# 32 steps of the second half's input projection ahead of the first half's mixers

## The chip, the cores and the metric

The kernel runs on one core of one Trainium2 chip. The metric is the device time of one execution in microseconds, median over several. A core has TensorE (PE, matrix multiply), VectorE (DVE), ScalarE (ACT), GpSimd (POOL) and SyncE (SP), which here issues the DMA transfers. Each engine takes its instructions strictly in the order in which they were put on it; an instruction that waits holds everything behind it on its engine.

## The reference

One step of a decoder layer over 2048 prompt tokens and 64 sample tokens (8 sequences of 8), model width 1024. Cut to what matters:

```python
h = rmsnorm(x) * (1 + sc1) + sh1
proj = h @ w_in                               # 1024 -> 2816 columns
qkv, z, b, a, sq, sk, sv = split(proj)
qkv = silu(causal_conv4(qkv))
o_dn = gated_delta_rule(qkv, b, a)            # 4 heads of 128, chunk by chunk
o_dn = rmsnorm(o_dn) * silu(z)
o_swa = window_attention(sq, sk, sv)          # 8 heads, window 128, sinks, bias
x = x + g1 * (concat(o_dn, o_swa) @ w_out)
h = rmsnorm(x) * (1 + sc2) + sh2
u = causal_conv3(h @ w_up)                    # 2 x 2816
x = x + g2 * ((silu(gate) * up) @ w_down)
y = rmsnorm(x)
```

## The kernel before, in words

Activations lie transposed, columns are tokens. All large products are split in three: an operand is a high part `hi` and a remainder `lo`, and one k of 8 takes three matmuls on PE, hi by hi, lo by hi, hi by lo. That is one *step* of a projection (`gemm_steps`). The tokens come in two halves: the first has two blocks of 512 columns, the second three of 384, 384 and 320 (`HALVES`), the last 64 of which are the sample tokens.

The input projection (`inproj`) has 22 weight tiles of 128 output columns. `project` takes pairs of weight tile m and block in the order that `pairs` gives: for the second half the first two weight tiles go together over the blocks, so that the order is (m0, b0), (m1, b0), (m0, b1), (m1, b1), (m0, b2) and so on. Each pair fills one PSUM tile `in_ps` in eight steps, 24 matmuls, from a pool of two banks, and `in_evac` then takes it away: for m below 12 a convolution of four taps (`conv_block`: ACT L538 and L541, three DVE L548), SiLU (L565, L566) and a store to `proj`.

The activations of the second half come from `affine_h`, called by `second` when the first half's projection has let a block's place go. For each block and k a tile `ht` is loaded (SP L264), scaled (DVE L265), and split into `hi` (ACT) and `lo` (DVE L272 or POOL L269 by turns). The 64 sample columns are loaded together as `hst` (SP L249) and worked on in four DVE steps (L252 to L256). `ht`, `hst` and the evacuations' `ev` share one tag, "cv", of five buffers.

The mixers of the first half (`mixers(0, mp)`) run chunks 0 to 7. For each chunk four generators go in lockstep: the state recurrence `scan` (s_ps, o_ps, p_ps), attention `attend` (as_ps, pt_ps, pv_ps; it loads kw, qs and sv), the triangular inverse of the next chunk `levels` (z_ps, u_ps, small tiles), and `front` two chunks ahead (kq_ps, d_ps, v_ps, am_ps; vb at L699 scales the values). `beside(steps, filler, share)` issues `share` filler steps behind each mixers step; `SHARE[1]` is 2.0, and the filler is the second half's input projection. When the mixers have been issued, `between(0, ...)` loads their result (`mix_load`: mt from `mixd`, split at L1171 and L1172) beside the rest of the in-projection (`in_end`), and then the out-projection (op_ps) begins.

The order in the program is a priority and not the order on the engines. The framework schedules ahead of time: by its own estimate of what is ready it picks, on each engine, the earliest instruction in the program that can go, and that fixes each engine's order. So what stands earlier in the program tends to go first where both are ready.

Of the kernel before, what the change touches and what calls it, by code (L numbers as in the profile page):

```python
# [96 lines left out]
def kernel(  # L97
# [7 lines left out]
    def new_pool(es, name, bufs=1, side="left", space=None):  # L105
        kw = {} if space is None else dict(space=space)
        return es.enter_context(tc.tile_pool(name=name, bufs=bufs, side=side, reuse_waits="tile", **kw))
# [218 lines left out]
    def load_split(src, eng=None, out=None):  # L326
        return split(load_raw(src), eng, out)
# [22 lines left out]
    def beside(steps, filler, share):  # L350

        due = 0.0
        for _ in steps:
            due += share
            while due >= 1:
                next(filler, None)
                due -= 1

    def lockstep(*gens):
        gens = list(gens)  # L360
        while gens:
            gens = [g for g in gens if next(g, None)]
            yield True
# [5 lines left out]
    def rest(steps):  # L369
        for _ in steps:  # L370
            pass

    def project(ms, src, load, hb, hf, evac, after=None, freed=None, tags=("acc",), turn=(2, 2), third=None, w0=None):


        order = list(pairs(ms, turn, len(HALVES[hf])))
        new = [m for i, (m, _) in enumerate(order) if m not in [x for x, _ in order[:i]]]
        first = max(2, turn[0])
        w = {m: w0 if w0 and not i else (load, third)[i == 2](m) for i, m in enumerate(new[:first])}
        new = new[first:]  # L380
        last = {bi: i for i, (_, bi) in enumerate(order)}
        for i, (m, bi) in enumerate(order):
            ps = bank(src, tags[i % len(tags)])
            yield from gemm_steps(ps, w[m], hb[bi], HALVES[hf][bi][1])
            end = bi == len(HALVES[hf]) - 1
            if end and new:
                w[new[0]] = load(new[0])
                new.pop(0)
            evac(m, bi, ps)
            if end and after:  # L390
                after(m)
            if freed and last[bi] == i:
                freed(bi)
# [197 lines left out]
    def in_evac(hf, bi, m, ps, ic):  # L591
        c0, n = HALVES[hf][bi]
        np_ = n - LS if c0 + n == LT else n
        ev = evp[0].tile([P, 512], F32, tag="cv", name="ev", bufs=evp[2])[:, :n]
        if m < 12:
            o = ic["out"]
            rb = conv_block(ps, n, np_, o[:, m, 0:3], b8(o[:, m, 3:27]), ic["cw"][:, m], None, ev)
            if TWICE[hf] == 2:
                silu2(ev, rb)
            else:  # L600
                nc.scalar.activation(ev, ev, AF.Silu)
        elif m < 16:
            nc.scalar.activation(ev, ps[:, :n], AF.Tanh, scale=0.5)
            nc.vector.scalar_tensor_tensor(ev, ev, 1.0, ps[:, :n], ALU.add, ALU.mult)  # L604
            nc.gpsimd.tensor_scalar(ev, ev, ic["dnw"], 1.0, ALU.mult, ALU.mult)
        elif m < 20:
            nc.scalar.mul(ev, ps[:, :n], -0.125)
        else:
            nc.scalar.copy(ev, ps[:, :n])
        nc.sync.dma_start(proj[m, :, c0:c0 + n], ev)  # L610
        if m == 20 and c0 + n == LT:
            nc.sync.dma_start(O["p_swa_k"], ev[:, np_ - P:np_])
            nc.sync.dma_start(O["s_swa_k_new"], ev[:, np_:])

    def inproj(hf, h, ic, ms, **kw):
        return project(ms, "in_ps", lambda m: load_split(I["w_inT"][m], nc.gpsimd if hf and m % 2 else nc.vector), h, hf,
                       lambda m, bi, ps: in_evac(hf, bi, m, ps, ic), **kw)
# [9 lines left out]
    def attn_consts(pool):  # L627
        NB = pool.tile([P, 8, P], F32, tag="NB", name="NB", bufs=1)
        t0 = toep[0]
        for v in range(2):  # L630
            t = pool.tile([P, 4, 256], F32, tag="kq", name="nbt", bufs=3)
            nc.sync.dma_start(t, bass.AP(t0.tensor, t0.offset + 4 * v * P * TOEP + 127, [[TOEP - 1, P], [P * TOEP, 4], [1, 256]]))
            nc.vector.tensor_tensor(NB[:, 4 * v:4 * v + 4], t[:, :, :P], t[:, :, P:], ALU.min)
        own = pool.tile([P, P], F32, tag="own_", name="own_", bufs=1)
        nc.vector.tensor_tensor(own, cst[:, C_TGT:C_TGT + P], ident, ALU.add)
        sink = pool.tile([P, 8], F32, tag="sink", name="sink", bufs=1)
        nsink = pool.tile([P, 8], F32, tag="nsink", name="nsink", bufs=1)
        nc.sync.dma_start(sink, I["sinks"].partition_broadcast(P))
        nc.vector.tensor_scalar_mul(nsink, sink, -1.0)
        return NB, own, sink, nsink  # L640
# [125 lines left out]
    def inverse_tiles(pool):  # L766

        inv[:] = [pool.tile([P, H, P], F32, tag=f"inv{i}", name=f"inv{i}", bufs=1) for i in range(2)]
        inv.append(pool.tile([P, H, 64], F32, tag="T64", name="T64", bufs=1))
        for t in inv:  # L770
            nc.gpsimd.memset(t, 0.0)
# [147 lines left out]
    def attend_load(c, pool):  # L919
        c0, k0 = P * c, P * (c == 0)  # L920

        qs = pool.tile([P, 4, P], F32R, tag="qs", name="qs", bufs=1)
        nc.sync.dma_start(qs.bitcast(F32), proj[16:20, :, c0:c0 + P].rearrange("m p t -> p m t"))
        kw = pool.tile([P, 256], F32R, tag="kw", name="kw", bufs=1)
        nc.sync.dma_start(kw[:, k0:].bitcast(F32), proj[20, :, c0 - P + k0:c0 + P])
        sv = pool.tile([P, P], F32, tag="sv", name="sv", bufs=1)
        nc.sync.dma_start(sv, proj[21, :, c0:c0 + P])
        return qs, kw, sv
# [456 lines left out]
    class Quarters:  # L1385
# [14 lines left out]
        def ahead(self, p, j):  # L1400

            J, end = len(self.order), MI - 1 - PLAIN
            i = J * (p - PLAIN) + j + RING
            if i < J * end:
                self.split(PLAIN + i // J, i % J)
            else:
                self.split(MI - 1, i - RING_T - J * end)
# [468 lines left out]
    with ExitStack() as main:  # L1876
# [95 lines left out]
        filler = inproj(0, h, ic, range(2, 12), tags=("acc", "acc", "fr", "fr", "at"), turn=(0, 0), w0=w2)  # L1972
# [16 lines left out]
        def mixers(hf, pool):  # L1989
            c0 = NCH // 2 * hf  # L1990
            c1 = c0 + NCH // 2
            ds = chunks
            at = attn_consts(pool)
            loaded = [attend_load(c0, pool)]
            for c in range(c0, c1):
                g = [scan(c, ds[c], pool), attend(c, c1, at, loaded, pool)]
                if c + 1 < c1:
                    g.append(levels(ds[c + 1], pool))
                if c + 2 < c1:
                    g.append(front(c + 2, ds[c + 2], pool))  # L2000
                yield from lockstep(*g)
# [10 lines left out]
        with ExitStack() as es:  # L2012
            mp = new_pool(es, "mp", bufs=2, side="right")
            filler = inproj(0, h, ic, range(12, 22), freed=second, turn=(0, 2))
            inverse_tiles(mp)
            beside(ahead(0, mp), filler, SHARE[0])
            rest(filler)
            g1 = gates(1, h1, ic["wb"], ip)
            filler = inproj(1, h1, ic, range(22), after=lambda m: m in range(2, 20) and next(g1, None))
            beside(mixers(0, mp), filler, SHARE[1])  # L2020
        uc = []

        def in_end():
            yield from filler
            nc.sync.dma_start(O["dn_conv"], ic["out"])
            states.close()
            uc.append(up_consts(new_pool(states, "up")))

        with ExitStack() as es:
            up_tags[:] = FREE_TAGS  # L2030
            filler, _ = between(0, in_end(), es, range(MU))
# [10 lines left out]
        with ExitStack() as es:  # L2042
            up_tags[:] = FREE_TAGS
            filler, h = between(1, filler, es, range(2 * PLAIN))
# [119 lines left out]
```

## Time and profile before

| | |
|---|---|
| median of 3 runs | 2659.92 us (2656.89 to 8718.18) |
| profiled execution | 2661.34 us |
| its span | 2659.2 us |
| mean granted TensorE clock | 0.99 |
| PE busy | 2583.2 us (97%), 16552 instructions |
| DVE busy | 1828.3 us (69%) |
| ACT busy | 1262.5 us (47%) |
| POOL busy | 752.7 us (28%) |

The span runs from the first to the last instruction of the profiled execution. Within it the mixers of the first half begin at about 355 us, their last matmul (ot_ps) is at 739.2 us, and the last in_ps of the second half ends at about 810 us, where the out-projection begins. Rows of the timeline give the start, the duration, the engine, the line, the operation, out<-in, and in square brackets the idle time before with what ended it.

### The profile page before, as it was taken

To read this page: it belongs to the slowest core of one execution; us is meant where nothing else is said; L and a number is where in the kernel's file an instruction comes from. 1 tells how busy PE (TensorE), PEld (TensorE's weight loads), DVE (VectorE), ACT (ScalarE), POOL (GpSimd) and SP (SyncE) were. 2 spreads that over 40 slices of the span, in tenths; PEclk is the share of its full clock that TensorE was granted. 3 is DMA by queue.
4 is the path that set the end of the run, shared out by engine and by line. 5 is a ranking of instruction groups with operands and counts; after the bars stand their busy time and mean duration, and the time that the engine had idled before them with its cause. 6 is when DMAs were issued, how large, how long until landed. Compare 5 with 4: busy or idle time off the path is not lost. (4 is left out here: it accounts for less than half of the span.)

```text
span 2659.2 us, 45647 instructions
## 1 busy us (share of the span) xinstructions
PE 2583.2 (97%) x16552; PEld 2231.5 (84%) x16552; DVE 1828.3 (69%) x3681; ACT 1262.5 (47%) x3081; POOL 752.7 (28%) x643
## 2 busy tenths in 40 slices
PE   6999989999999899999999999999999999999998
PEld 5677877887898787777777779999999997889988
DVE  6475469988422678878857665786777666677676
ACT  5453255555232445545444454555555553554343
POOL 2032134332331422323111113345555520021022
PEclk9999989999999999999999999999999999999999
DMA  7787343332255343333226447424555458678673
GB/s 278 247 302 233 114 128 114 86 101 85 87 167 182 116 136 87 84 102 95 77 86 202 148 156 245 135 74 154 172 175 183 167 183 293 211 237 283 218 247 133
DMA packets 305791, 433.58 MB, mean 163 GB/s; under 512 B 81779, under 2 KB 189012, under 8 KB 305300
## 3 DMA queue, kind: packets, MB, share of 16 engines
q1 hardware_dynamic: 305564, 430.66, 49.7%
q8 instruction: 130, 2.13, 0.3%
q14 instruction: 97, 0.79, 0.1%
HBM read 316.25 MB, written 115.33 MB: 162 GB/s over the span
## 5 line engine op out<-in xcount | busy, mean ns | idle before, releaser
L340 PE MATMUL in_ps<-hi,w_hi 128*128 128x512 f32 (+2 forms) x880 | 317.6, 364 | 9.5 <-DVE ev L604 4.7
L340 PE MATMUL up_ps<-hi,w_hi 128*128 128x512 f32 (+2 forms) x808 | 316.4, 392 | 7.3 <-ACT cv L543 7.3
L340 PE MATMUL in_ps<-lo,w_hi 128*128 128x512 f32 (+2 forms) x880 | 318.4, 362 | 2.7 <-DVE lo L272 1.7
L340 PE MATMUL in_ps<-hi,w_lo 128*128 128x512 f32 (+2 forms) x880 | 315.9, 359 | 0.0
L340 PE MATMUL up_ps<-lo,w_hi 128*128 128x512 f32 (+2 forms) x808 | 312.9, 387 | 0.0
L340 PE MATMUL up_ps<-hi,w_lo 128*128 128x512 f32 (+2 forms) x808 | 311.7, 387 | 0.0
L1784 PE MATMUL dn_ps<-th,wh 128*128 128x512 f32 (+2 forms) x796 | 272.3, 343 | 5.4 <-DVE x L1252 3.5
L1784 PE MATMUL dn_ps<-tl,wh 128*128 128x512 f32 (+2 forms) x796 | 272.6, 343 | 3.5 <-DVE tl L1676 3.5
L1784 PE MATMUL dn_ps<-th,wl 128*128 128x512 f32 (+2 forms) x796 | 271.2, 342 | 0.0
L332 DVE TENSOR_TENSOR w_lo<-w_raw,w_hi 128x1024 fp32r<-128x1024 f32 x115 | 143.4, 1247 | 110.8 <-ACT w_hi L331 109.0
L331 ACT CAST w_hi<-w_raw 128x1024 fp32r<-128x1024 f32 x126 | 132.1, 1048 | 161.6 <-PE op_ps L340 58.7
L340 PEld LDWEIGHTS in_ps<-hi,w_hi 128*128 128x128 f32 x880 | 166.7, 190 | 31.9 <-issue 5.1
L340 PEld LDWEIGHTS up_ps<-hi,w_hi 128*128 128x128 f32 x808 | 152.3, 188 | 46.3 <-issue 11.4
L340 PEld LDWEIGHTS in_ps<-lo,w_hi 128*128 128x128 f32 x880 | 167.1, 190 | 26.6 <-issue 7.6
L340 PEld LDWEIGHTS in_ps<-hi,w_lo 128*128 128x128 f32 x880 | 167.1, 190 | 16.1 <-issue 1.6
L340 PEld LDWEIGHTS up_ps<-lo,w_hi 128*128 128x128 f32 x808 | 152.4, 189 | 33.2 <-issue 8.5
L340 PEld LDWEIGHTS up_ps<-hi,w_lo 128*128 128x128 f32 x808 | 152.3, 189 | 30.6 <-issue 4.0
L1784 PEld LDWEIGHTS dn_ps<-th,wh 128*128 128x128 f32 x796 | 150.9, 190 | 22.6 <-DVE x L1252 4.8
L1784 PEld LDWEIGHTS dn_ps<-tl,wh 128*128 128x128 f32 x796 | 151.1, 190 | 19.4 <-DVE tl L1676 3.8
L1784 PEld LDWEIGHTS dn_ps<-th,wl 128*128 128x128 f32 x796 | 151.0, 190 | 15.5
L1675 ACT CAST wh<-wr 128x512 fp32r<-128x512 f32 x149 | 92.1, 618 | 144.8 <-PE dn_ps L1784 113.9
L548 DVE SCALAR_TENSOR_TENSOR ev<-rb,cw,ev 128x512 f32<-128x512 f32 (+2 forms) x180 | 131.4, 734 | 26.9 <-ACT ev L541 25.1
(546 smaller groups left out, 6488.5 us busy)
## 6 DMA issues: line engine op xcount, KB each, us to landing
w_raw<-in_w_upT_dram SPq DMA_DIRECT2D x50, 512.0 KB
wada<-in_w_ada_dram SPq DMA_DIRECT2D x48, 512.0 KB
w_raw<-in_w_inT_dram SPq DMA_DIRECT2D x44, 512.0 KB
wr<-ws_d SPq DMA_DIRECT2D x88, 256.0 KB
w_raw<-in_w_outT_dram SPq DMA_DIRECT2D x34, 512.0 KB
d<-act_d SPq DMA_DIRECT2D x33, 512.0 KB
wr<-in_w_downT_dram SPq DMA_DIRECT2D x66, 256.0 KB
tr<-T_d SPq DMA_DIRECT2D x66, 256.0 KB
```

Of the source, the lines that this page charges most:

```text
L331: nc.scalar.copy(hi, raw)
L332: (eng or nc.vector).tensor_tensor(lo, raw, hi.bitcast(F32), ALU.subtract)
L340: nc.tensor.matmul(ps[:, :n], a[:, k, :], b[:, k, :n], start=first is not False and k == ks[0] and i == 0, stop=last is not False and k == ...
L548: nc.vector.scalar_tensor_tensor(out, src(j), w[:, j:j + 1], out, ALU.mult, ALU.add)
L1675: nc.scalar.copy(h, raw)
L1784: nc.tensor.matmul(acc[m, s][:, :n], w[q, i][a][:, c], th[b][:, v], start=new and i == 0 and y == 0, stop=i == KH - 1 and y == 2, skip_gro ...
```

## The change

Between the making of the filler and `beside`, 32 filler steps are issued at once, then the mixers begin as before.

```diff
             g1 = gates(1, h1, ic["wb"], ip)
             filler = inproj(1, h1, ic, range(22), after=lambda m: m in range(2, 20) and next(g1, None))
+            for _ in range(32):
+                next(filler)
             beside(mixers(0, mp), filler, SHARE[1])
```

A PSUM tile takes eight steps, so these are four tiles: weight tiles 0 and 1 on the first block and on the second. No instruction is added or taken away on any engine; only the order differs. The orders agree up to the start of the mixers, differ from there to the end of the in-projection, and agree again from the out-projection's first matmul on.

On PE, at the start of the first half's mixers, before: two in_ps steps stand between the inverse (z_ps), and the attention scores (as_ps) and the recurrence (s_ps) follow.

```order
L780 MATMUL z_ps<-T_2270,AM 32x16 x5
L340 MATMUL in_ps<-hi,w_hi 128x384
L340 MATMUL in_ps<-lo,w_hi 128x384
L340 MATMUL in_ps<-hi,w_lo 128x384
L340 MATMUL in_ps<-hi,w_hi 128x384
L340 MATMUL in_ps<-lo,w_hi 128x384
L340 MATMUL in_ps<-hi,w_lo 128x384
L780 MATMUL z_ps<-T_2270,AM 32x16 x11
L667 MATMUL kq_ps_3557<-cst,kq 128x128 x3
L959 MATMUL as_ps<-kh,qh 128x128
L959 MATMUL as_ps<-kw,qh 128x128
L868 MATMUL s_ps<-u,Kt 128x128 x4
```

Now the 48 matmuls of the first block stand there in one piece, but for s_ps; these are the last of them and what follows on PE.

```order
L340 MATMUL in_ps<-hi,w_hi 128x384
L340 MATMUL in_ps<-lo,w_hi 128x384
L340 MATMUL in_ps<-hi,w_lo 128x384
L959 MATMUL as_ps<-kh,qh 128x128
L959 MATMUL as_ps<-kw,qh 128x128
L959 MATMUL as_ps<-kh,qs 128x128
L959 MATMUL as_ps<-kh,qh 128x128
L959 MATMUL as_ps<-kw,qh 128x128
L959 MATMUL as_ps<-kh,qs 128x128
L780 MATMUL z_ps<-T_2270,AM 32x16 x11
L667 MATMUL kq_ps_3705<-cst,kq 128x128 x4
L880 MATMUL o_ps<-u,AM 128x128 x4
```

All of as_ps but its first group, z_ps, kq_ps and o_ps have moved behind the first block's in_ps.

Some seventy rows further on PE, where the third chunk's front reaches am_ps, before: the inverse and the rest of the attention come next, and in_ps of the second block only behind kq_ps.

```order
L697 MATMUL v_ps<-cst,xv 128x128 x4
L706 MATMUL am_ps_3774<-kq 128x256 x2
L780 MATMUL u_ps<-inv_2269,Y 32x32 x8
L780 MATMUL u_ps<-Y,inv_2269 32x32 x4
L706 MATMUL am_ps_3807<-kq 128x256 x2
L986 MATMUL pt_ps<-cst,nl 128x128 x8
L667 MATMUL kq_ps_3960<-cst,kq 128x128 x4
L340 MATMUL in_ps<-hi,w_hi 128x384
```

Now:

```order
L780 MATMUL u_ps<-inv_2269,Y 16x16 x16
L780 MATMUL u_ps<-Y,inv_2269 32x16 x12
L686 MATMUL d_ps<-gm,tgtr 128x512 x2
L697 MATMUL v_ps<-cst,xv 128x128 x4
L706 MATMUL am_ps_3935<-kq 128x256 x2
L340 MATMUL in_ps<-hi,w_hi 128x384
```

The 48 matmuls of the second block begin right behind the first am_ps; z_ps, pt_ps, ot_ps, u_ps and the second am_ps have moved behind them.

On SP's queue at the same place, the loads of the activations, before: the load of kw (which overwrites a buffer that attention reads) stands ahead of hst and of the third block's ht.

```order
L264 DMA ht<-in_xT_dram 128x384 x4
L925 DMA kw<-proj 128x256
L249 DMA hst<-in_xT_dram 128x8x64
L923 DMA qs<-proj 128x4x128
L264 DMA ht<-in_xT_dram 128x256 x3
```

Now:

```order
L264 DMA ht<-in_xT_dram 128x384 x4
L249 DMA hst<-in_xT_dram 128x8x64
L264 DMA ht<-in_xT_dram 128x256 x4
L925 DMA kw<-proj 128x256
L923 DMA qs<-proj 128x4x128
```

The load of hst and four loads of ht have moved ahead of kw. On DVE the steps on hst move up in the same way: L252 now stands right behind the last affine rows of the second block and ahead of Y (L788), and L699 (vb) comes 34 rows behind it.

## Prediction

> **What bounds the kernel now.** First the page's busy shares, then the stage in 50 us windows, because a share over the whole span hides where TensorE (PE) stands still.
>
> ```profile
> PE 2583.2 (97%) x16552; PEld 2231.5 (84%) x16552; DVE 1828.3 (69%) x3681; ACT 1262.5 (47%) x3081; POOL 752.7 (28%) x643
> ```
>
> PE is busy 2583.2 of 2659.2 us, so only 76 us of the span are not PE work. A change that adds and removes no instruction can win by two things alone: less idle PE, and less PE time at half clock. The windows (duration; busy time and count of PE, PEld, DVE, ACT, POOL; granted PE clock; DMA share; GB/s) show where both lie near the edit:
>
> ```profile
> 350.00:400.00 50.00, 42.74 (x308) 36.68 (x307) 41.59 (x90) 31.55 (x104) 22.83 (x18) 0.76 0.39 117
> 400.00:450.00 50.00, 47.60 (x325) 40.08 (x323) 47.97 (x131) 27.95 (x104) 22.67 (x19) 1.00 0.36 104
> ```
>
> The first row is the hole: 7.26 us without PE work and a mean clock of 0.76. There the first half's mixers begin, and the second half's input projection has only just got its first activations. PE's waits from 355 to 395 us, by what ended them, hold all of that idle time:
>
> ```profile
> PE am_ps L706 <- DVE vb L699: 4.1, 1, 4.1
> PE as_ps L959 <- DVE nl L969: 2.8, 1, 2.8
> PE in_ps L340 <- ACT ev L609: 0.4, 1, 0.4
> ```
>
> The clock is read from windows of 1 us:
>
> ```profile
> 362.00:363.00 1.00, 1.00 (x6) 0.88 (x5) 1.00 (x7) 0.87 (x6) 0.00 (x0) 0.51 0.83 198
> 379.00:380.00 1.00, 1.00 (x7) 1.00 (x7) 1.00 (x5) 1.00 (x4) 0.00 (x0) 0.95 0.00 1
> 385.00:386.00 1.00, 0.00 (x0) 0.00 (x0) 1.00 (x2) 0.51 (x1) 1.00 (x1) 0.96 0.83 225
> 392.00:393.00 1.00, 1.00 (x6) 0.71 (x5) 1.00 (x3) 0.09 (x1) 0.81 (x1) 0.63 0.26 76
> ```
>
> A window with mean clock c that switches between 1 and 0.5 switches at a point found from c: the clock falls at 362.0, rises at 379.1, falls at 385.9 and rises at 392.7. These stand 17.1, 6.8 and 6.8 us apart, all close to multiples of 3.41 us. The first half-clock stretch follows the 2.8 us wait, and lasts while PE runs small tiles; the second follows the 4.1 us wait. PE's timeline (start, duration, engine, line, tile, shape, count, [idle before <- releaser]) gives the price:
>
> ```profile
> 361.78 0.32 PE L959 MATMUL as_ps<-kh,qh 64*128 64x128 f32 x1 [2.80 <-DVE nl L969]
> 362.20 2.07 PE L868 MATMUL s_ps<-u,Kt 128*128 128x128 f32 x8
> 374.20 0.52 PE L340 MATMUL in_ps<-hi,w_lo 128*128 128x384 f32 x1
> 374.52 0.52 PE L340 MATMUL in_ps<-hi,w_hi 128*128 128x384 f32 x1
> 382.93 0.44 PE L780 MATMUL z_ps<-T,AM 32*32 32x32 f32 x16
> 388.01 2.08 PE L706 MATMUL am_ps<-kq 128*128 128x256 f32 x4 [4.06 <-DVE vb L699]
> 390.83 2.06 PE L706 MATMUL am_ps<-kq 128*128 128x256 f32 x4
> 392.70 1.07 PE L986 MATMUL pt_ps<-cst,nl 128*128 128x128 f32 x8
> 393.60 0.60 PE L667 MATMUL kq_ps<-cst,kq 128*128 128x128 f32 x4
> 393.96 0.42 PE L340 MATMUL in_ps<-hi,w_hi 128*128 128x384 f32 x1
> 394.39 0.34 PE L340 MATMUL in_ps<-hi,w_lo 128*128 128x384 f32 x1
> 394.56 0.35 PE L340 MATMUL in_ps<-hi,w_hi 128*128 128x384 f32 x1
> ```
>
> Start to start, an in_ps matmul takes 0.32 us at half clock (374.20 to 374.52) and 0.17 at full (394.39 to 394.56). Half of the busy half-clock time, (17.1 + 6.8 - 2.1 idle) / 2, is 10.9 us; with 7.3 us idle the hole costs 18 us. That is the most the start region can return.
>
> **The change, part by part.** The edit issues 32 filler steps, three matmuls each, ahead of the first mixers step: 96 in_ps matmuls, 96 x 0.173 = 16.6 us of PE work, that before stood among the mixers and behind them. They are four PSUM tiles: both weight tiles on the first 384-column block (48 matmuls), then both on the second (48). Moving full PE work only changes the time where it fills a hole or opens one.
>
> *First block.* Its activations are ready, so 48 matmuls run from 356.9 in one piece at 0.173 us, with s_ps among them (eight passes, 2.07 us at half clock, 1.0 at full): 8.3 + 1.0 us, to about 366.2. The 2.8 us wait goes, and with it the fall of the clock at 362.0. What is late next: the gate and attention matmuls that stood here come behind the block: some 26 at 0.13 us each, by the s_ps row at full clock, so they finish about 370.
>
> *The activations behind it.* In the new order the load of the sample columns (hst) stands right behind four ht loads on SP's queue, no longer behind a load of kw that waits for an attention buffer. The rows of SP, DVE, POOL and ACT before:
>
> ```profile
> 362.21 4.53 SPq L264 DMA_DIRECT2D ht<-in_xT_dram  x4
> 372.62 0.33 SPq L925 DMA_DIRECT2D kw<-proj  x1
> 372.99 0.44 SPq L249 DMA_DIRECT2D hst<-in_xT_dram  x1
> 378.09 0.69 DVE L252 TENSOR_TENSOR hst<-hst,MOD 128x512 f32<-128x512 f32 x1 [2.76 <-DMA hst<-in_xT_dram]
> 378.70 0.42 DVE L940 TENSOR_TENSOR kw<-kw,kh 128x256 fp32r<-128x256 f32 x1
> 387.27 0.69 DVE L699 TENSOR_TENSOR vb<-v_ps,nr 128x512 f32<-128x512 f32 x1
> 392.91 0.58 ACT L541 ACTIVATE ev<-in_ps,cw 128x384 f32<-128x384 f32 x1 [0.92 <-POOL lo L269]
> ```
>
> The ht loads end at 366.7, so hst starts near 367.3 instead of 373.0. It took 378.09 - 372.99 = 5.1 us to reach VectorE, which now takes it near 372.4. But VectorE stands on it with the mixers' Y (L788) queued behind, so PE idles from about 370.3 to 373.4, 3 us: the new wait. Behind it PE has u_ps, d_ps and v_ps, about 2.5 us, and then am_ps, which needs vb. Between hst and vb VectorE's order holds 34 rows. The groups of its kinds from 355 to 395 (count, busy us, mean ns) price the largest:
>
> ```profile
> L265 DVE SCALAR_TENSOR_TENSOR ht<-ht,MOD,sg 128x256 f32<-128x256 f32 x8 | 4.4, 563 | 0.0
> L972 DVE CUSTOM_DVE_ANT_0 nl<-nl,NB,nsink 128x128 f32<-128x128 f32 x8 | 2.5, 348 | 0.1
> L693 DVE TENSOR_SCALAR nr<-nr 128x4 f32<-128x4 f32 x1 | 1.2, 1225 | 0.0
> ```
>
> Three steps on hst (0.69 each) are 2.1, five of L265 2.8, six of L972 2.1 (their readouts 0.5 more), L693 1.2, and the other 13 I put at 6: 14.7 us. A row starts about 0.08 us before the one ahead ends (378.78 against 378.70), which takes 2.5 off. So vb begins some 12 us behind hst, near 384, and am_ps near 384.6, against 388.0. This estimate carries the sum.
>
> *Second block.* Its first matmul stands right behind am_ps: 384.6 + 2.1 = 386.7, against 393.96. It needs one of two PSUM banks, freed by the first evacuation (L541), which waits for a buffer of the five it shares with the activations: before, for the POOL subtraction (L269) that ends at 392.9; after, for the one of hst (L256), two rows ahead of vb. So that evacuation comes near 383.5, and doesn't hold the block. [...]
>
> [...]
>
> *The account at 396.2.* Before had issued 61 in_ps by then (54 up to 395.0):
>
> ```profile
> 355.00:395.00 40.00, 13.93 (x54) 0.70 0.41 128
> 690.00:810.00 120.00, 109.94 (x642) 1.00 0.45 133
> ```
>
> (PE's in_ps alone: busy time and count, clock.) After has 96, so 35 x 0.173 = 6.1 us ahead. It has not done z (0.44), u (about 0.45), the second am (1.0 at full clock), pt (1.07) and kq (0.4): 3.4 us behind. Net gain 2.7 us. Ends: with am_ps at 382 it is some 5 us and with VectorE never waiting for hst about 9; with vb still at 387.3 and L541 at 392.9, the block starts at 394 and the sum is a loss of about 5, to 8 with the clock. I take 2.7.
>
> *From 396 to the mixers' end.* The same work in another order. Windows of all engines:
>
> ```profile
> 395.00:470.00 75.00, 70.78 (x551) 60.46 (x550) 72.06 (x217) 42.81 (x158) 32.58 (x27) 1.00 0.38 109
> 470.00:600.00 130.00, 129.90 (x1150) 109.52 (x1149) 116.65 (x334) 70.46 (x260) 50.11 (x42) 1.00 0.33 93
> 600.00:690.00 90.00, 86.42 (x674) 71.72 (x672) 75.31 (x223) 42.15 (x137) 31.75 (x28) 1.00 0.28 79
> ```
>
> PE is idle for 4.2 + 0.1 + 3.6 = 7.9 us. VectorE is 96% busy in the first window, and the four evacuations come earlier:
>
> ```profile
> L548 DVE SCALAR_TENSOR_TENSOR ev<-rb,cw,ev 128x384 f32<-128x384 f32 x21 | 15.9, 762 | 0.1
> ```
>
> Three of 0.76 us are 2.3 us a tile, of which the two tiles on the second block come new ahead of the mixers' rows. Bounds: all idle gone, -7.9; the two tiles' 4.6 us as a new wait of PE, +4.6. Work is displaced both ways, so I take 0.
>
> *The tail.* From 690 to 810 PE does almost nothing but in_ps, 642 of them; 96 fewer remain. What that work hides is the reload of the mixers' result:
>
> ```profile
> L910 PE MATMUL ot_ps<-cst,o x4: 272/272/273, 738.8 to 739.2; 128*128 128x128 f32 x4
> L1171 ACT CAST mixh<-mt x16: 606/620/623, 746.3 to 770.1; 128x512 fp32r<-128x512 f32 x16
> ```
>
> It ends 31 us behind the last mixers matmul. The mixers end 16.6 - 2.7 = 14 us later, the reload near 785, and the in-projection near 807: 22 us of cover are left. Cost 0. From the out-projection's first matmul the orders are the same.
>
> **Sum.** The profiled execution took 2661.34 us; less 2.7 gives 2658.6. The median of the runs shown, 2659.92, is 1.4 lower, and would give 2657.2. I say 2658.
>
> **The rivals.** *The hole really closes.* If hst lands early enough, and VectorE reaches vb much sooner than in my 12 us, PE keeps dense 128x384 work, the clock stays up, and most of the 18 us return: 8 to 16 us, 2645 to 2653. For it: 48 matmuls stand in one piece where the first gap was. Against it: am_ps stays behind v_ps and vb, a chain on four engines that no in_ps fills. *Slower.* PE takes its queue in order, so 48 matmuls of the second block in front of z, pt and the first chunk's output hold the mixers if they wait. If VectorE or the five shared buffers bring vb or L541 as late as before, the block starts near 394 and everything of the mixers comes 8 us later, with a second cold start: 5 to 11 us, 2664 to 2672. The point from which it decides is a block start at 389.5, 2.8 us behind my estimate. *No effect.* The affine chain through the five buffers (13 ht loads and hst from 355 to 390) sets when both blocks can go, whatever stands ahead in the program; fills and waits trade, within 2 us: 2659 to 2663.
>
> **How the numbers follow.** Forecast (2653 to 2662, gains up to 8 with the downstream term) 48%; the hole closes 20%; slower 22%; no effect 10%. The range that holds 8 in 10 leaves out the outer halves of the first two rivals: 2646 to 2669. Two per cent, 53 us, is about what a measurement of this kernel can tell from no change. The hole holds 18 us and the slower mechanism 11, so within 2% has 0.97; 0.01 is left for faster and 0.02 for slower, where the cover of the tail would have to break as well.
>
> **What the changed profile would show.** Right: no as_ps wait and clock 1.00 at 362; a PE wait near 370 that ends with VectorE's Y; hst issued near 367; am_ps near 384.6 and the second block near 386.7, with clock 1.00 from 389 or 393; mixers' last ot_ps near 753; out-projection's first matmul near 807.5 instead of 810.3. Wrong: a second block after 389.5; a clock that stays full through 370 to 385; or PE idle from 396 to 750 that differs by more than 6 us from the 7.9 here.

## The result, and the profile after

The changed kernel took 2665.9 us (median of 6; 2660.86 to 2668.09) against 2656.35 us for the kernel before measured with it: ratio 1.0029, 95% interval 1.0015 to 1.0043. By the ratio that is 8 us slower (the medians lie 9.55 us apart), within 2%, and on the other side of the forecast. One execution of before, at 8718.18 us, is not in the ratio. The profiled executions stand closer, 2662.73 against 2661.34 us, and why is half of this story.

The page of the changed kernel, its busy time, on every engine within 4 us of before:

```profile
PE 2579.2 (97%) x16552; PEld 2228.0 (84%) x16552; DVE 1831.6 (69%) x3681; ACT 1263.6 (47%) x3081; POOL 749.5 (28%) x643
```

The windows that answer to those of before (duration; busy time and count by engine; granted PE clock; DMA share; GB/s):

```profile
350.00:400.00 50.00, 38.36 (x306) 34.81 (x305) 46.40 (x96) 32.66 (x101) 23.38 (x18) 0.83 0.38 117
400.00:450.00 50.00, 50.00 (x326) 40.63 (x324) 46.16 (x128) 29.44 (x107) 21.74 (x19) 1.00 0.39 111
395.00:470.00 75.00, 74.18 (x611) 62.46 (x609) 69.37 (x203) 44.97 (x162) 29.89 (x25) 1.00 0.41 117
470.00:600.00 130.00, 121.08 (x999) 101.17 (x999) 115.59 (x321) 64.57 (x230) 44.43 (x39) 0.99 0.32 87
600.00:690.00 90.00, 86.69 (x721) 71.77 (x720) 76.47 (x236) 42.89 (x150) 30.99 (x27) 1.00 0.30 85
```

The start is a hole again, with more idle time (11.6 us) and a higher clock; the first window behind it is fuller than before; and from 470 to 600 us PE, which stood still for 0.1 us before, stands still for 8.9. PE's waits in the start, from 355 to 395 us:

```profile
PE am_ps L706 <- DVE vb L699: 6.8, 1, 6.8
PE v_ps L697 <- ACT Dc L689: 2.0, 1, 2.0
PE as_ps L959 <- DVE nl L969: 1.4, 1, 1.4
PE u_ps L780 <- DVE Y L788: 1.3, 1, 1.3
```

and the rows that the forecast's steps name, of SP, DVE, ACT and PE:

```profile
367.29 0.38 SPq L249 DMA_DIRECT2D hst<-in_xT_dram  x1
370.45 1.19 DVE L252 TENSOR_TENSOR hst<-hst,MOD 128x512 f32<-128x512 f32 x1 [0.83 <-DMA hst<-in_xT_dram]
383.25 0.69 DVE L699 TENSOR_TENSOR vb<-v_ps,nr 128x512 f32<-128x512 f32 x1
383.18 0.58 ACT L541 ACTIVATE ev<-in_ps,cw 128x384 f32<-128x384 f32 x1 [0.77 <-DVE lo L256]
384.00 2.08 PE L706 MATMUL am_ps<-kq 128*128 128x256 f32 x4 [6.80 <-DVE vb L699]
385.51 0.88 PE L340 MATMUL in_ps<-hi,w_hi 128*128 128x384 f32 x1
395.56 0.44 PE L780 MATMUL z_ps<-T,AM 32*32 32x32 f32 x16
```

hst at 367.3, am_ps at 384.0 (384.6 said), the second block from 385.5 to 395.6 (386.7 to 396.2 said): the start went as it was worked out. The rest did not.

To compare many traces, one stretch serves: from the first 128x384 matmul of in_ps to the out-projection's first matmul. From windows of 1 us its length is split into three parts: PE idle; PE busy at half clock, counted as busy time x (1 - clock); and the work left at full clock. Where a kernel was traced more than once, each trace has its number.

| | ratio to before, 95% interval | stretch | first 40 us: idle + half-clock loss | then to 690 us: idle | half-clock loss |
|---|---|---|---|---|---|
| before | | 453.4, 454.9, 447.6, 447.1 | 17.7, 18.7, 10.1, 9.9 | 7.9, 6.4, 7.7, 7.6 | 0, 1.7, 0, 0 |
| changed (32) | 1.0029 [1.0015, 1.0043] | 455.9, 458.2, 461.0 | 15.5, 14.8, 15.1 | 13.1, 12.6, 13.0 | 1.7, 5.1, 5.1 |
| 8 steps | 1.0038 [1.0026, 1.0050] | 460.0 | 13.7 | 11.5 | 6.7 |
| 16 | 1.0041 [1.0029, 1.0053] | 460.8 | 14.7 | 8.4 | 4.9 |
| 24 | 0.9995 [0.9987, 1.0004] | 447.2, 446.6 | 14.4, 14.2 | 8.4, 8.1 | 1.7, 1.7 |
| 28 | 1.0039 [1.0025, 1.0053] | 460.4 | 15.7 | 7.8 | 8.2 |
| 48 | 1.0027 [1.0014, 1.0041] | 457.3 | 14.2 | 8.6 | 6.7 |
| 32, then pause | 1.0045 [1.0031, 1.0059] | 460.6 | 14.5 | 9.0 | 3.4 |
| 32, late | 1.0031 [1.0017, 1.0044] | 458.5 | 12.2 | 9.5 | 1.7 |
| 32, share 1.9 | 1.0053 [1.0038, 1.0067] | 466.6 | 14.5 | 10.9 | 11.5 |
| 32, share 2.1 | 1.0008 [0.9998, 1.0017] | 453.7 | 13.7 | 4.6 | 1.7 |
| 24, share 2.1 | 1.0004 [0.9992, 1.0016] | 453.2 | 14.8 | 9.8 | 4.6 |
| before, split of tile 1 on DVE | 1.0040 [1.0027, 1.0053] | 456.1 | 12.7 | 11.1 | 4.4 |

The stretch's means are 450.8 us before and 458.4 after, 7.6 us apart, about the whole measured loss. This mean counts four traces of before alike, two of 454 and two of 447 us; how often each kind comes is not known.

### The profile page after: what moved, and what is told of

Its sections match the earlier page's. It is cut to its first block, busy times and chain, and to the rows that moved or that the text cites. A ratio compares the mean times of both kernels' runs of the same rounds, so it can differ in the third digit from the quotient of the medians.

```text
span 2661.0 us, 45652 instructions
## 1 busy us (share of the span) xinstructions
PE 2579.2 (97%) x16552; PEld 2228.0 (84%) x16552; DVE 1831.6 (69%) x3681; ACT 1263.6 (47%) x3081; POOL 749.5 (28%) x643
## 4 chain that ended last, share of the span: by engine, by line
PE 63%; DVE 5%; DMA 3%; ACT 1%; issue 1%; SPq 0%; POOL 0%; POOLq 0%; DVEq 0%; ACTq 0%
PE up_ps L340 19%; PE dn_ps L1784 14%; PE op_ps L340 6%; PE uq_b L1574 5%; PE in_ps L340 3%; PE uq_c L1574 3%; PE uq_u L1574 2%; PE uq_g L1574 2%; PE uq_a L1574 1%; DMA tr<-T_d 1%; PE pv_ps L996 1%; PE as_ps L959 1%; PE am_ps L706 1%; PE u_ps L780 1%; DMA mt<-mixd 0%
## 5 line engine op out<-in xcount | busy, mean ns | idle before, releaser
L332 DVE TENSOR_TENSOR w_lo<-w_raw,w_hi 128x1024 fp32r<-128x1024 f32 x115 | 142.0, 1235 | 100.2 <-ACT w_hi L331 98.3
L1784 PEld LDWEIGHTS dn_ps<-th,wl 128*128 128x128 f32 x796 | 151.2, 190 | 15.5
L1676 DVE TENSOR_TENSOR wl<-wr,wh 128x512 fp32r<-128x512 f32 x149 | 109.0, 732 | 55.8 <-ACT wh L1675 54.6
```

The costliest lines, as they stand in the source:

```text
L332: (eng or nc.vector).tensor_tensor(lo, raw, hi.bitcast(F32), ALU.subtract)
L1676: nc.vector.tensor_tensor(l, raw, h.bitcast(F32), ALU.subtract)
L1784: nc.tensor.matmul(acc[m, s][:, :n], w[q, i][a][:, c], th[b][:, v], start=new and i == 0 and y == 0, stop=i == KH - 1 and y == 2, skip_gro ...
```

## The experiments

**Both kernels again.** Unchanged, three more traces of before and two more of the changed kernel in all.

> The kernel before once more, beside itself. All theories: a ratio of 1.000 within 0.15%. It gives a second trace of before and the granted clock of several executions. 'Clock by chance' (the change costs nothing between 355 and 811 us beyond the 2 us that the first pair of traces shows, and the rest of the 7.7 us is PE time at half clock that differs from execution to execution): the clock here is 0.990 to 0.992 in all executions, and higher than in the changed kernel. 'Downstream order' (the start gains about 3 us, the mixers' rest loses about 6): PE idle between 396 and 690 us again near 8 us.

> The changed kernel once more. All: ratio near 1.003. 'Downstream order': PE idle between 396 and 690 us again near 13 us, with PE waiting for xz (L911) for 3 us or more, and again one fall of the clock or more in that stretch. 'Clock by chance': the idle time between 396 and 690 differs from the first trace by several us, or the out-projection begins within 1 us of before and the rest is lost behind it.

Before: ratio 0.9995 [0.9982, 1.0008]; changed: 1.0029 [1.0014, 1.0044]. PE's idle time from 396 to 690 us came back as in the first traces of each, and with it the wait for xz. The second trace of the changed kernel, PE's waits from 396 to 690 us:

```profile
PE p_ps L853 <- DVE xz L911: 5.9, 2, 3.8
PE pt_ps L986 <- DVE nl L979: 2.3, 1, 2.3
```

So these gaps belong to the order and not to the execution. In this trace the clock also fell at 578 us for 6.8 us, behind the second wait for xz, where the first trace has no fall: that part is the execution's. A third trace of the changed kernel:

> The changed kernel a third time, for one more trace. 'Downstream order': PE again idle for 12 to 14 us between 396 and 690 us, with the waits for xz near 520 and 577 us. 'More falls of the clock in most executions': granted clock 0.986 to 0.989 in this one, and the falls that the first two traces lack lie right behind the waits of PE between 396 and 690 us; a clock of 0.991 would tell nothing.

2668.68 us at a clock of 0.989, with 13.0 us idle, falls at 527 and 581 us, and one more at 783 us, in the tail. The falls are where they were expected, but for that one.

**Start or rest.** Two kernels take the change apart. One makes the start of the change and then lets 16 mixers steps pass without filler, so that the filler is where before has it; the other has the start of before and issues the 32 steps after 16 mixers steps.

```diff
+            first = mixers(0, mp)
+            for _ in range(16):
+                next(first)
-            beside(mixers(0, mp), filler, SHARE[1])
+            beside(first, filler, SHARE[1])
```

> 32 steps ahead as in the change, and then 16 mixers steps without filler, so that the filler stands where before has it again. The start of the change with the pacing of before. 'Downstream order': 2 to 4 us faster than before (the start's gain alone). 'The start costs' (the account at 396 us is wrong, and holding the mixers behind the second block is what is paid for): 5 to 9 us slower, like the change.

```diff
-            for _ in range(32):
-                next(filler)
-            beside(mixers(0, mp), filler, SHARE[1])
+            first = mixers(0, mp)
+            beside((next(first) for _ in range(16)), filler, SHARE[1])
+            for _ in range(32):
+                next(filler)
+            beside(first, filler, SHARE[1])
```

> The first 16 mixers steps with their filler as before, then the 32 steps at once, then on as in the change: the start of before with the pacing of the change. 'Downstream order': slower than before by 4 to 10 us, and PE idle between 396 and 690 us well over 8 us. 'The start costs': within 2 us of before, with PE idle there near 8 us.

Both are slower, 1.0045 and 1.0031, and neither theory has both: the pause loses 12 us, more than either expected, and the late one loses 8 us as "downstream order" had it, but with 9.5 us idle, only 2 more than before. The pause doesn't give back before's order: the work left at full clock is 432.8 us there and 430.8 in the late one, against 426 to 428 before. PE's small matmuls stand in other groups among the long ones. Most of the pause's 5 us lies in the attention scores: the same 168 matmuls of as_ps keep PE busy for 23.74 us before and for 27.87 with the pause (and for 19.88 with 24 steps, below). PE's as_ps alone from 395 to 810 us, in these three in turn:

```profile
395.00:810.00 415.00, 23.74 (x168) 1.00 0.36 105
395.00:810.00 415.00, 27.87 (x168) 0.99 0.36 104
395.00:810.00 415.00, 19.88 (x168) 1.00 0.37 107
```

Whether the grouping makes the time of these matmuls was not taken apart. What the pair shows is that neither start nor pacing alone brings back the time of before.

**How many steps.** Only the number is changed, `range(32)` to 8, 16, 24, 28 and 48.

> 8 steps ahead in place of 32: one tile, (weight tile 0, first block). 'Downstream order' in its plain form (the start gains, and any new order of the mixers' rest has gaps of its own that have nothing to do with the number of steps): anything from 2 us faster to 12 slower, told by PE's idle time between 396 and 690 us beside the 8 us of before. 'The lead is the price' (every step of lead holds the mixers back, and that is never made up): about 2 us slower, a quarter of the change's loss.

> 16 steps ahead: both weight tiles on the first block alone; the second block stays among the mixers. 'Downstream order': the first wait (2.8 us) and the fall of the clock at 362 us go as in the change, which is worth 3 to 8 us at the start, and the rest is again told by the idle time between 396 and 690 us. 'The lead is the price': about 4 us slower. 'The second block is the price' (48 matmuls in front of the inverse and the attention of the next chunk): faster than before by 2 us or more.

> 24 steps ahead: the first block and one weight tile on the second. 'Downstream order': no place of its own between 16 and 32. 'The lead is the price': about 6 us slower, between 16 and 32. 'The second block is the price': half of the change's loss, 4 us slower.

> 28 steps ahead, between the 24 that cost nothing and the 32 of the change: the first block, one tile on the second block and half of the next one. 'Downstream order': no value between the two is owed; 2 us faster to 12 us slower, told by the idle time behind 396 us. 'The second block is the price': 3 to 5 us slower.

> 48 steps ahead: all three blocks of two weight tiles. 'Downstream order': no trend, again told by PE's idle time behind 396 us. 'The lead is the price': 10 to 14 us slower. 'The second block is the price': like the change or a little more, 8 to 10 us slower.

8 and 16 are slower by 10 us, 24 costs nothing, 28 is slower by 10 again, 48 by 7. "The lead is the price" and "the second block is the price" both fall: 16 has no second block in front and is slow, 24 has half of it and is not. The start is nearly the same in all five, 13.7 to 15.7 us; what moves the time is behind it. Windows from 396 to 690 us, of 24 steps:

```profile
396.00:690.00 294.00, 285.59 (x2376) 239.95 (x2375) 263.34 (x761) 152.33 (x545) 113.87 (x93) 0.99 0.34 96
```

and of 8:

```profile
396.00:690.00 294.00, 282.53 (x2273) 236.65 (x2272) 265.69 (x758) 150.80 (x541) 112.42 (x88) 0.98 0.33 93
```

DVE and the others do nearly the same work; with 8 steps PE is idle for 3 us more and, by the table, loses 5 us more to half clock. Idle time alone does not tell the slow ones: 16, 28 and 48 steps stand still for 7.8 to 8.6 us, hardly more than before, and lose 4.9 to 8.2 us by half clock. Nor is 24 good because its waits are gone, for its idle time and half clock are 2 us above before's. Its work left at full clock is 421.7 us in both traces against 427.1 before, 5 us less, and as_ps has 4 of them. No step of any theory had said so: 24 is a lucky order.

**The same start with another pacing.** The change with `SHARE[1]` 1.9 and 2.1 in place of 2.0; the first rows of PE's order, through the start, are those of the change.

> The change (32 steps ahead) with 1.9 filler steps to a mixers step in place of 2.0, so that the start stays as in the change and only the pacing behind it differs. 'Downstream order' (the start gains 2 to 5 us whatever follows; PE's gaps behind 396 us belong to the single order): the time moves by several us either way against the change, with PE's idle time between 396 and 690 us, and the wait for am_ps near 384 us stays. 'The lead is the price': 7 to 9 us slower than before, as the change.

> The change with 2.1 filler steps to a mixers step in place of 2.0. As for 1.9: 'downstream order' has several us of difference from the change, told by PE's idle time between 396 and 690 us; 'the lead is the price' has 8 to 10 us slower than before.

1.0053 and 1.0008. At the same lead the pacing behind it is worth 12 us. Windows of 1.9 and of 2.1 from 396 to 690 us:

```profile
396.00:690.00 294.00, 283.12 (x2301) 239.24 (x2299) 256.79 (x736) 149.95 (x541) 105.26 (x89) 0.96 0.32 92
```

```profile
396.00:690.00 294.00, 289.37 (x2444) 243.05 (x2443) 262.22 (x771) 153.01 (x551) 108.64 (x93) 0.99 0.34 97
```

With 2.1 PE is idle for 4.6 us, less than before, and yet the kernel does not beat before: its tail has 6.1 us of idle time.

**Is the hole of before always there?** The sum put 18 us on the start of before. Two more traces of it:

> The kernel before a third time, for a trace. 'The traces of before were slow ones': at a granted clock of 0.991 or more, the stretch from the first 128x384 matmul to the out-projection takes 449 to 452 us instead of 453.4 and 454.9, with less than 24 us at half clock in its first 40 us. 'The rest of the loss lies behind the out-projection': again 453 to 455 us.

> The same once more, for a fourth trace of before: the same two expectations.

2655.59 and 2651.22 us, at clocks of 0.993 and 0.994, and stretches of 447.6 and 447.1 us, below both expectations: the start is another one. PE's waits from 350 to 400 us in the third trace, and its rows of DVE and POOL from 358 us:

```profile
PE z_ps L780 <- DVE T L801: 4.0, 1, 4.0
PE am_ps L706 <- DVE vb L699: 2.7, 1, 2.7
PE as_ps L959 <- DVE nl L969: 0.3, 1, 0.3
358.05 1.91 DVE L265 SCALAR_TENSOR_TENSOR ht<-ht,MOD,sg 128x384 f32<-128x384 f32 x2 [0.75 <-DMA ht<-in_xT_dram]
359.51 2.67 POOL L332 TENSOR_TENSOR w_lo<-w_raw,w_hi 128x1024 fp32r<-128x1024 f32 x1
359.88 0.43 DVE L969 COPY_PREDICATED nl<-own__3428,as_ps 128x256 f32<-128x256 uint32 x1
360.35 1.98 DVE L972 CUSTOM_DVE_ANT_0 nl<-nl,NB,nsink 128x128 f32<-128x128 f32 x1
```

The L265 and L332 rows in the trace on which the forecast was built:

```profile
357.55 3.83 DVE L265 SCALAR_TENSOR_TENSOR ht<-ht,MOD,sg 128x384 f32<-128x384 f32 x2 [1.30 <-DMA ht<-in_xT_dram]
358.31 2.65 POOL L332 TENSOR_TENSOR w_lo<-w_raw,w_hi 128x1024 fp32r<-128x1024 f32 x1
```

Two affine rows take 1.9 us where the second is under way before GpSimd's split starts, and 3.8 where it comes behind: it ends 0.4 us behind the split (361.4 and 361.0). By itself that second row takes 1.22 us in the one and 2.69 in the other. L969, for whose result as_ps waits, comes right behind it. In the third and fourth traces a row beside the split is longer too, but one behind L969: the first L972 takes 1.98 and 1.97 us there and ends 0.15 and 0.14 us behind the split, and takes 0.35 in the forecast's trace. "The meeting" below is that of the split with the second L265 row, in the first two traces. Under a microsecond decides. In the one case as_ps waits 0.3 us and the clock stays at 1.00 until 376 us; in the other it waits 2.8 us, and 17 us of half clock follow, with 7 more behind the wait for am_ps. Windows of the third trace and of the first, 355 to 395 us:

```profile
355.00:395.00 40.00, 32.88 (x298) 27.80 (x297) 38.49 (x87) 28.89 (x99) 21.36 (x17) 0.87 0.45 137
```

```profile
355.00:395.00 40.00, 32.74 (x257) 28.48 (x255) 32.25 (x79) 25.10 (x85) 15.13 (x12) 0.70 0.41 128
```

The same idle time, but a clock of 0.87 and not 0.70.

To see whether this meeting makes the long wait, GpSimd's split of that one tile was given to VectorE in the kernel before:

```diff
-        load_split(I["w_inT"][m], nc.gpsimd if hf and m % 2 else nc.vector)
+        load_split(I["w_inT"][m], nc.gpsimd if hf and m % 2 and m > 1 else nc.vector)
```

> The kernel before, with the split of the second half's weight tile 1 (w_lo, L332) on VectorE in place of GpSimd, so that no GpSimd row of 2.7 us stands beside the affine rows at 358 us. 'The meeting makes the slow form': in the trace the two L265 rows take 1.3 us, PE's wait for as_ps there is below 1.5 us (the split now costs VectorE 1.2 us there) and the clock does not fall before 370 us. 'The slow form has another cause': a wait of 2 us or more and a fall near 360 us as in the first traces. The whole time says little, since the order behind changes as well: 5 us faster to 12 slower.

PE's waits of that kernel from 350 to 400 us:

```profile
PE z_ps L780 <- DVE T L801: 4.6, 1, 4.6
PE in_ps L340 <- ACT ev L541: 1.6, 1, 1.6
PE am_ps L706 <- DVE vb L699: 1.4, 1, 1.4
PE o_ps L880 <- DVE S L871: 0.5, 1, 0.5
PE as_ps L959 <- DVE nl L969: 0.2, 1, 0.2
```

The long wait for as_ps and the 17 us of half clock are gone, though the clock falls at 366 us for 3.4 us, earlier than expected, and at 380 us for 6.8; the two L265 rows took 1.7 us, where 1.3 was expected. One trace, where two of four traces of before have neither the long wait nor the 17 us by themselves, agrees with the meeting and does not prove it. The order behind changed as well, and the kernel is slower, 1.0040.

**Two that were good.** 24 steps again, and with the pacing of 2.1:

> 24 steps ahead once more: if it was no chance of the executions, a ratio of 0.998 to 1.001 to before and a stretch from the first 128x384 matmul to the out-projection of 446 to 450 us. If it was chance, 1.003 and 457 us or more.

> 24 steps ahead and 2.1 filler steps to a mixers step. 'Downstream order': another order again, between 4 us faster and 10 slower, told by PE's idle time and half clock behind 396 us; that each of the two was good by itself is no reason that both together are.

0.9994 [0.9983, 1.0004] and 1.0004 [0.9992, 1.0016]. 24 steps stay where they were, 1.5 us below before and not to be told from it; with 2.1 there is nothing on top. No version here beats the kernel before beyond its interval.

## Why the prediction was wrong

**The start.** First block without a wait, clock 1.00 at 362, hst near 367, am_ps near 384.6, second block near 386.7: each came within 1.2 us, but that PE's idle time in front of u_ps was 1.3 and in front of the attention 1.4 us, where one wait of 3 us was said, and that a wait of 2.0 us for v_ps was not foreseen. That vb came so near its time has some luck in it: hst reached VectorE at 370.45, 2 us earlier than said, and from there to vb it took 12.8 us, 0.8 more. That the second block ends at 396.2, where the account is drawn, was the author's estimate, and no run shows it: in the changed trace the clock was 0.70 from 388 to 389 us and 1.00 from there, and the block ended at 395.6. Nor did the half clock of before last with small tiles alone: PE was busy for all 17.0 us from 362 to 379 at 0.50, the last 4.9 of them on in_ps. The account of 2.7 us also holds against the trace it was made from: idle and half clock in the first 40 us are 15.1 us on average in the three traces after, against 17.7. But that trace had the meeting. Over four traces before has 14.1 on average, and 10.0 in the two without the meeting. The gain of the start is then a loss of 1 us, and of 5 against those two: the changed kernel has a wait of 6.8 or 6.9 us for am_ps and 17 us of half clock around it in all three traces, before without the meeting 10 us of half clock. How often before meets is not known: its traces with the meeting have a mean clock of 0.990 and 0.989, those without 0.993 and 0.994, and of its 118 executions with a clock on record 39 have 0.990 or less, 14 have 0.993 or more, and 65 lie between. This is the first step that failed: the 18 us were read from one execution, and the gain of 2.7 us measured as a loss of 1.

**From 396 to the mixers' end.** "Work is displaced both ways, so I take 0", with bounds of -7.9 and +4.6. Measured: idle 7.4 us before and 12.9 after, +5.5; and half clock 0.4 before, 4.0 after, +3.5. Together +9, twice the upper bound. This is the second step that failed, and the larger: the term taken as 0. Two things were left out. The bound counted DVE's evacuations alone and left out falls of the clock, though at before's start one had come right behind a wait (2.8 us for as_ps, then a clock of 0.51 from 362 to 363 us). And it was not the evacuations of the second block that made PE wait: the window to 450 us is full. The long wait comes at 520 us. PE's row, and some of DVE's and POOL's rows ahead of it:

```profile
523.68 1.16 PE L853 MATMUL p_ps<-S,kq 128*128 128x128 f32 x8 [3.80 <-DVE xz L911]
514.13 2.39 DVE L733 TENSOR_TENSOR gt<-G,TU 32x48 f32<-32x48 f32 x1
517.01 1.00 DVE L566 SCALAR_TENSOR_TENSOR ev<-rb,ev 128x384 f32<-128x384 f32 x1
517.93 1.50 DVE L548 SCALAR_TENSOR_TENSOR ev<-rb,cw,ev 128x256 f32<-128x256 f32 x1
519.36 1.29 DVE L548 SCALAR_TENSOR_TENSOR ev<-sb,cw,ev 128x64 f32<-128x64 f32 x1
520.57 1.27 DVE L735 TENSOR_TENSOR TU<-TU,gt 32x48 f32<-32x48 f32 x1
521.84 0.47 DVE L548 SCALAR_TENSOR_TENSOR ev<-rb,cw,ev 128x256 f32<-128x256 f32 x1
522.43 0.20 DVE L733 TENSOR_TENSOR gt<-G,TU 32x55 f32<-32x55 f32 x1
522.66 0.24 DVE L735 TENSOR_TENSOR TU<-TU,gt 32x55 f32<-32x55 f32 x1
522.94 0.69 DVE L911 TENSOR_TENSOR xz<-ot_ps,xz 128x512 f32<-128x512 f32 x1
513.63 2.82 POOL L332 TENSOR_TENSOR w_lo<-w_raw,w_hi 128x1024 fp32r<-128x1024 f32 x1
516.56 1.03 POOL L659 TENSOR_TENSOR gm<-cst,ghl 128x512 fp32r<-128x512 f32 x1
517.56 3.01 POOL L991 TENSOR_TENSOR PT<-pt,cst 128x512 f32<-128x512 f32 x2
520.53 1.26 POOL L690 TENSOR_TENSOR Dc<-Dc,cst 128x512 f32<-128x512 f32 x1
```

The same DVE form takes 0.47 us at 521.84, where POOL has no row, and 1.50 while POOL multiplies PT; the stretched rows end from 0.05 to 0.4 us behind a POOL row. L911, on which PE stands, comes behind them: what it reads, ot_ps, was ready by 515.8, and VectorE is busy without a gap of 0.1 us until it takes L911. Five stretched rows (L733, L566, two L548, L735) take 7.5 us together; an estimate from the unstretched rows of this trace (L733 0.20, L566 0.47, L548 0.47 and 0.27, L735 0.24) has 1.7, so some 5.8 us were lost ahead of a wait of 3.8. The 32 steps of lead put the filler's splits and evacuations elsewhere against the mixers' POOL rows, and here a split, gm, two PT rows and Dc follow one another ahead of xz. That a different pacing removes the idle time is shown (2.1: 4.6 us); that this meeting is the cause of this wait is read from the trace and was not tried by itself.

**The tail.** The mixers' last ot_ps came at 753.6 (753 said), the reload ended near 783 (785 said), and its cover held. The out-projection began at 811.3, 813.5 and 819.6 instead of 807.5; nearly all of that comes from ahead. That the mixers' end came on time in the first trace is luck: "96 fewer remain" was said of in_ps, and behind the last ot_ps there are 347 against before's 413, 66 fewer. The other 30, some 5 us at 0.173, had slipped behind the mixers, which left room for the lost time ahead of the mixers' end.

**The work at full clock** is 424.7 us on average after and 427.1 before: 2.4 us less, a gain that no step had. So 1.0 + 5.5 + 3.5 - 2.4 gives the 7.6 us of the stretch, the tail being equal.

**The rivals.** "Slower" had 5 to 11 us, and that is the size, but by another way: it was to decide by a second block later than 389.5, and that came at 385.5. "The hole really closes" fell, for the reason given against it: am_ps waits for vb. "No effect", within 2 us, fell too.

## What to carry to other kernels

Before a gain is read from a hole in one trace, look at that hole in two or three: here the 17 us of half clock behind a 2.8 us wait were in two of four traces, and against the other two the change's start lost 5 us. Moving work in a program whose order a scheduler makes gives every engine another order behind the move; beside a tuned kernel, bound that by more than the idle time that stands there, and add falls of the clock behind new waits (1.7 to 5.1 us lost from 396 to 690 us in the changed kernel's three traces) and the time that the same small matmuls take in another order (as_ps: 19.9 to 27.9 us here). Try neighbours of the number before judging the idea: 24, 28 and 32 steps differed by 10 us with the same start.

## What was not expected of the hardware

Some DVE rows that met a POOL row were not just a little longer, and ended 0.05 to 0.4 us behind that row: 0.47 us became 1.50, and L735, 0.24 us on 55 columns two microseconds later, took 1.27 on 48. Not all were: L969 took 0.43 us beside the split, and 0.43 where the split was VectorE's. And in the same kernel, on one core, a meeting that turns on less than a microsecond went with a stretch that was 7 us longer (453.4 and 454.9 us against 447.6 and 447.1), with 10.9 and 11.3 us lost to half clock in its first 40 us against 3.1 and 3.0.
